# Attention and hyena stage of a hybrid block: another order within each attention step, four buffers for the hyena rows, and a step for the context keys

## The chip, the cores and the metric

The kernel runs on one core of a Trainium2 chip. The metric is device microseconds from start to end of the one launch; several runs are taken and their median stands for the kernel. Engines are named as in the profile: PE is TensorE, DVE is VectorE, ACT is ScalarE, POOL is GpSimd, SP is SyncE, which issues most of the DMAs.

## The reference

One layer of a diffusion backbone over 1024 latent tokens of width 1024, with 256 context tokens. A normalised and modulated input goes through one projection, whose columns feed neighbourhood attention (8 heads of 64, window 8 by 16 on a 16 by 64 grid, plus all context keys) and a two-step hyena long convolution; both are projected, gated and merged, and a SwiGLU network follows.

```python
h = modulate(rmsnorm(x, norm1_g[i]), sh1, sc1)
q, k, v, hv, hx1, hx2, gna, ghy = jnp.split(h @ w_in[i], IN_SPLITS, axis=-1)
y_na = neighbourhood_attention(to_heads(q), to_heads(k), to_heads(v),
                               to_heads(k_c), to_heads(v_c), na_rpb[i])
y_hy = hyena_mixer(hv, hx1, hx2, *hy_params)
x = x + g1 * gated_merge(gna, ghy, y_na, y_hy, w_na_o[i], w_hy_o[i], w_out[i])
# in neighbourhood_attention: s_nb = q_rot.k_band * scale + bias ; s_ctx = q.k_ctx * scale
#   p = softmax(concat(s_nb, s_ctx)) ; o = p_nb @ v_band + p_ctx @ v_ctx
# in gated_merge: m = sigmoid(g_na)*(y_na @ w_na_o) + sigmoid(g_hy)*(y_hy @ w_hy_o)
```

Everything is float32. The kernel gets that accuracy from TensorE by splitting each operand x into a high part (a cast by ACT, L178) and a low part (a subtraction by DVE, L179) and by three products (low weight by high x, high by low, high by high) for each product of the reference.

## The kernel before

The program runs through stages: modulation and first norm; the input projection, woven with the hyena filters and long convolutions; attention, woven with the rest of the projection and then with the hyena output projection; the merge and output projection; the SwiGLU network. The change touches the attention stage, which lies at 618 to 892 us of the span, and what is prepared for it.

**Items and steps.** Attention is cut into 32 items: 4 pairs of heads, 2 row blocks, 4 column blocks. Each item has 128 queries for two heads against 640 keys (384 of the window, 256 of the context). The generator `attention` makes one step for each item, and two more steps at the end. Step it issues, in this order on PE:

- scores of item it (`scores`, matmuls at L971 and L974, 12 of them, with 64-row tiles), into two PSUM tiles s_ps;
- turns of item it-1 (`turn`, L991): ten 128 by 128 transposes of the normalised probabilities pe into columns 0:1280 of the one PSUM tile pt_ps (a pool with a single buffer, 1536 columns of float32);
- values of item it-2 (`values`, L1005): 20 matmuls with 128 by 64 tiles from pts, the SBUF copy of the turned probabilities, into columns 1280:1408 of the same pt_ps;
- then a product: in the first 18 steps (items 0 to 17) 24 matmuls of the input projection into in_ps, after that 12 matmuls of the hyena output projection into hy_ps (both by `gemm`, L200).

DVE adds the bias to the scores and finds the maxima (L979, one instruction for each head), and scales by the reciprocal sum (L983, L984). ACT takes the exponentials (L980, two for an item, each followed by a read of its sum), copies the turned part of pt_ps to pts (L995 in `turned_out`), copies the values from pt_ps into a row of yrow (L1012 in `row`), and evicts the projection (L780). Both also do the splits of weights, queries, keys and rows (L178, L179). When a row block of yrow is full, it is split into yah and yal.

**What sets the order.** PE's instructions in this stage are pinned (`keep_in_program_order`), and so is each split passed a pin; the other instructions are placed on their engines by the framework's scheduler when the program is built. From then on each engine runs its list in order and waits on semaphores. Where an order is shown below, it is this built list. The main loop, from which each step's product follows its attention part, is

```python
while self.left:
    next(attention)
    next(proj)
...
for _ in attention:
    next(hyena, None)
```

**Preparation.** The generator `operands` loads and turns the next keys and queries (load, shuffle, two multiplications, an addition, then splits), one piece per step; six pieces run before the first item. The raw tiles have two buffers, and a load is issued when one is taken out.

**Hyena rows.** `hyena_out` reads eight rows yhraw (four channel blocks, two halves of the tokens) from memory through two buffers, splits them into yhh and yhl, which lie in the buffers that the projection's input occupied, and then runs eight output blocks f by two halves h, 12 matmuls each. The rows for the second half are split with a pin, the last two of them in the step of f=0, h=1, which is their first use.

Of the kernel before, what the change touches and what calls it, by code (L numbers as in the profile page):

```python
# [161 lines left out]
class Block:  # L162
# [696 lines left out]
    def attention(self, pool, kpool, prep, psums):  # L859
# [13 lines left out]

        jobs = [(nm, pr, h) for pr in range(4) for nm, h in (("k", 0), ("k", 1), ("kc", 0), ("q", 0), ("q", 1))]
        raws = []
# [39 lines left out]
        def keys(pr):  # L915
            tl = tiles[pr]
            tl["kr"] = [prep.tile([P, T], F32R, tag=n, name=n, bufs=2) for n in ("krh", "krl")]
            tl["kc"] = [prep.tile([P, TC], F32R, tag=n, name=n, bufs=2) for n in ("kch", "kcl")]
            for h in range(2):
                sl = slice(512 * h, 512 * h + 512)  # L920
                for n, x in enumerate(turned(sl, False)):
                    if n:
                        self.split(tl["kr"][0][:, sl], tl["kr"][1][:, sl], x)
                if h:
                    x = raws.pop(0)
                    fetch()
                    self.split(*tl["kc"], x[:, 0:TC])
                yield

        def queries(pr, h):  # L930
# [7 lines left out]
        def operands():  # L938
# [4 lines left out]
            yield from queries(0, 0)  # L943
            for pr in range(4):
                yield from queries(pr, 1)
                if pr < 3:
# [46 lines left out]
        def turned_out(pt):  # L993
            pts = pool.tile([P, 2, 640], F32, tag="pts", name="pts", bufs=2)
            nc.scalar.copy(pts.rearrange("p a b -> p (a b)"), pt[:, 0:1280])  # L995
            return pts
# [19 lines left out]
        prepared = operands()  # L1016
        for _ in range(6):
            next(prepared)
        yield
        pss, pst = psums()  # L1020
        one, two = {}, {}
        for it in range(len(items) + 2):
# [3 lines left out]
            pt = pst.tile([P, 1536], F32, tag="t", name="pt_ps")  # L1026
            pes = one.pop(it - 1, None)
            if pes:
                turn(pes, pt)
            if it >= 2:  # L1030
                values(two.pop(it - 2), pt, *items[it - 2])
            if pes:
                two[it - 1] = turned_out(pt)
            if it >= 2:
                row(pt, *items[it - 2])
            yield
# [11 lines left out]
    def hyena_out(self, pool, wpool, ps1):  # L1048

        nc, a = self.nc, self.a  # L1050
        yh = [pool.tile([P, 8, 512], F32R, tag=n, name=m).rearrange("p (c h) t -> p c (h t)", h=2)
              for n, m in (("hTh", "yhh"), ("hTl", "yhl"))]
        parts = [(c, h) for h in range(2) for c in range(4)]
        loaded = []

        def load(n):
            for c, h in parts[len(loaded):len(loaded) + n]:
                raw = self.stg.tile([P, 4, P], F32, tag="tm", name="yhraw").rearrange("p a b -> p (a b)")
                nc.sync.dma_start(raw, self.yhd[c][:, h * 512:(h + 1) * 512])
                loaded.append((c, slice(h * 512, (h + 1) * 512), raw))  # L1060
# [4 lines left out]

        load(2)
        yield
        for n in (0, 2):
            split(n)
            load(2)  # L1070
            yield
        split(4, self.tc.keep_in_program_order)
        load(2)
        w = self.weights(wpool, a["why"][0], 512)
# [125 lines left out]
    def run(self):  # L1200
        tc, nc, a = self.tc, self.nc, self.a
        with ExitStack() as top:
# [21 lines left out]
            with ExitStack() as s1:  # L1224
# [56 lines left out]
                prep, attk = side_pool("prep", bufs=2), side_pool("attk", bufs=1)  # L1281
                attention = self.attention(side_pool("att", bufs=2), attk, prep, psums)
                next(attention)
                for _ in range(AHEAD):
                    next(proj)
# [503 lines left out]
```

## Time and profile before

| | us |
|---|---|
| median of three runs | 1675.22 (1674.61 to 1676.2) |
| the profiled execution | 1675.84 |
| its span | 1674.1 |
| mean granted TensorE clock | 0.994 |

| engine | busy us | share |
|---|---|---|
| PE | 1646.1 | 98% |
| PE's weight loads | 1306.8 | 78% |
| DVE | 1229.4 | 73% |
| ACT | 696.6 | 42% |
| POOL | 150.0 | 9% |

The page lists busy time, then groups of instructions with their mean duration in ns and the idle time in front of them, with what ended it. A timeline row gives start, duration, engine, line, instruction, output and inputs, and in brackets the idle time ahead of it on its engine. Durations of matmuls that follow each other overlap in these rows, so distances between starts are used here for PE.

### The profile page before, as it was taken

The numbers are of one execution on the slowest core, as the hardware profiler recorded it, in microseconds if no ns is written. First come the engines' busy times: TensorE is split into PE (matmuls) and PEld (weight loads), VectorE is DVE, ScalarE is ACT, GpSimd is POOL, SyncE is SP. The second block draws the span as 40 slices with busy tenths as digits, with TensorE's granted clock in tenths as the row PEclk, the third lists the DMA queues.
The fourth block names the chain that finished last, engine by engine and source line by source line (L and its number), as shares of the span: only waits on it lengthen the run. The fifth ranks groups of instructions, "written<-read, shape, count | busy, mean of one in ns | idle before, by whom it ended". The sixth has DMA issues, their size and how long they took to land.

```text
span 1674.1 us, 22694 instructions
## 1 busy us (share of the span) xinstructions
PE 1646.1 (98%) x8168; PEld 1306.8 (78%) x8168; DVE 1229.4 (73%) x2079; ACT 696.6 (42%) x1217; POOL 150.0 (9%) x274
## 2 busy tenths in 40 slices
PE   8999999999999999999999999999999999999998
PEld 6777777777777778887787888888888888888886
DVE  5866799799999774647765868878866666489576
ACT  6553343222212146445553317632333333355455
POOL 1020001000000050202000001001100111000000
PEclk9999999999999999999999999999999999999999
DMA  9754455645555383446447514434432323395344
GB/s 363 246 173 162 162 165 177 212 159 182 194 179 189 128 249 105 133 129 180 160 143 271 176 41 179 141 119 133 142 104 95 101 102 119 114 360 193 100 121 157
DMA packets 107637, 274.37 MB, mean 164 GB/s; under 512 B 14687, under 2 KB 23811, under 8 KB 105221
## 3 DMA queue, kind: packets, MB, share of 16 engines
q1 hardware_dynamic: 87992, 212.14, 38.0%
q0 software_dynamic: 19168, 60.11, 10.6%
q8 instruction: 65, 1.06, 0.3%
q10 hardware_dynamic: 365, 0.67, 0.1%
q14 instruction: 47, 0.39, 0.1%
HBM read 205.48 MB, written 67.39 MB: 163 GB/s over the span
## 4 chain that ended last, share of the span: by engine, by line
PE 52%; issue 11%; DMA 2%; POOL 1%; DVE 1%; SPq 0%; ACT 0%; POOLq 0%; DVEq 0%
PE x_ps L1459 14%; PE z_ps L1459 6%; PE dx_ps L1647 6%; PE out_ps L1397 5%; PE in_ps L200 4%; PE dz_ps L1647 4%; PE hy_ps L200 3%; PE y_ps L1459 2%; PE dy_ps L1647 2%; PE na_ps L200 2%; PE pt_ps L1005 1%; PE pt_ps L991 1%; POOL v L909 1%; PE s_ps L971 1%; PE dft_ps L604 1%
## 5 line engine op out<-in xcount | busy, mean ns | idle before, releaser
L200 PE MATMUL in_ps<-hTh,wl 128*128 128x512 f32 x576 | 232.6, 404 | 1.6 <-ACT proj L780 1.6
L200 PE MATMUL in_ps<-hTh,wh 128*128 128x512 f32 x576 | 228.0, 396 | 0.0
L200 PE MATMUL in_ps<-hTl,wh 128*128 128x512 f32 x576 | 226.8, 394 | 0.0
L200 PEld LDWEIGHTS in_ps<-hTh,wl 128*128 128x128 f32 x576 | 108.2, 188 | 26.8 <-issue 3.1
L200 PEld LDWEIGHTS in_ps<-hTh,wh 128*128 128x128 f32 x576 | 108.2, 188 | 23.6 <-issue 0.3
L200 PEld LDWEIGHTS in_ps<-hTl,wh 128*128 128x128 f32 x576 | 108.3, 188 | 21.8
L178 ACT CAST wh<-wr 128x1024 fp32r<-128x1024 f32 (+1 forms) x60 | 52.7, 878 | 139.7 <-PE in_ps L200 106.4
L179 DVE TENSOR_TENSOR wl<-wr,wh 128x1024 fp32r<-128x1024 f32 (+1 forms) x60 | 60.4, 1007 | 66.9 <-ACT wh L178 66.7
L179 DVE TENSOR_TENSOR ol<-ws,oh 128x512 fp32r<-128x512 f32 x88 | 60.2, 688 | 50.6 <-ACT oh L178 50.5
L179 DVE TENSOR_TENSOR ol<-ar,oh 128x512 fp32r<-128x512 f32 x77 | 52.7, 687 | 39.1 <-ACT oh L178 39.0
L178 ACT CAST oh<-ar 128x512 fp32r<-128x512 f32 x77 | 47.9, 622 | 78.6 <-PE dx_ps L1647 29.2
L178 ACT CAST oh<-ws 128x512 fp32r<-128x512 f32 x88 | 54.6, 622 | 55.9 <-PE x_ps L1459 26.7
L979 DVE CUSTOM_DVE_ANT_0 pe<-s_ps,bias 128x640 f32<-128x640 f32 x64 | 50.6, 820 | 32.2 <-PE s_ps L974 32.2
L980 ACT ACTIVATE pe<-pe,mx 128x640 f32<-128x640 f32 x64 | 52.7, 824 | 48.4 <-DVE mx L979 48.3
L1647 PE MATMUL dx_ps<-ol,oh 128*128 128x512 f32 x176 | 68.7, 391 | 0.0
L1647 PE MATMUL dx_ps<-oh,ol 128*128 128x512 f32 x176 | 68.2, 390 | 0.4 <-DMA ar<-g 0.2
L1647 PE MATMUL dx_ps<-oh 128*128 128x512 f32 x176 | 68.5, 389 | 0.0
L604 PE MATMUL dft_ps<-a,matf 128*128 128x512 f32 x128 | 67.1, 605 | 1.1 <-ACT dec L509 0.5
L178 ACT CAST oh<-wr 128x512 fp32r<-128x512 f32 x70 | 43.3, 621 | 54.2 <-PE x_ps L1459 18.4
L179 DVE TENSOR_TENSOR ol<-wr,oh 128x512 fp32r<-128x512 f32 x70 | 47.9, 688 | 21.8 <-ACT oh L178 21.7
L1399 DVE TENSOR_TENSOR x<-x,out_ps 128x512 f32<-128x512 f32 x64 | 43.0, 685 | 20.3 <-PE out_ps L1397 19.4
L647 ACT COPY bp<-dft_ps 128x512 f32<-128x512 f32 x16 | 9.4, 588 | 104.1 <-PE dft_ps L606 100.2
(424 smaller groups left out, 4354.5 us busy)
## 6 DMA issues: line engine op xcount, KB each, us to landing
wr<-in_w SPq DMA_DIRECT2D x52, 512.0 KB, 3.5
ar<-g SPq DMA_DIRECT2D x77, 256.0 KB, 3.1
wr<-in_w_in SPq DMA_DIRECT2D x36, 512.0 KB, 3.8
matf<-in_dft_f SPq DMA_DIRECT2D x32, 384.0 KB, 3.6
bias<-in_rpb SPq DMA_DIRECT2D x64, 192.0 KB, 3.5
g<-t POOLq DMA_DIRECT2D x47, 256.0 KB, 3.0
w<-in_w SPq DMA_DIRECT2D x44, 256.0 KB, 5.4
x<-in_x SPq DMA_DIRECT2D x16, 512.0 KB, 7.8
```

The costliest lines, as they stand in the source:

```text
L178: pin(self.nc.scalar.copy(hi, src))
L179: pin(self.nc.vector.tensor_sub(lo, src, hi.bitcast(F32)))
L200: mm = nc.tensor.matmul(ps, ww[:, k * P:(k + 1) * P], xx[:, k, pos:pos + width], start=(i == 0), stop=(i == n - 1))
L604: nc.tensor.matmul(ps, m[:, 0], v.rearrange("p a b -> p (a b)"), start=True, stop=False)
L909: nc.gpsimd.dma_start(v[32 * r:32 * r + 32].rearrange("p (a b) f -> p a b f", b=4)[:, :, cb, :], vg[:, CBASE[cb]:CBASE[cb] + 32, fs].rearr ...
L971: pin(nc.tensor.matmul(ps[:, 512:896], qs[qq], kw[kk], start=(i == 0), stop=(i == 2)))
L979: nc.vector.tensor_tensor_reduce(pe, ps[:, 256:896], bt, -1.0, 3e38, ALU.add, ALU.min, mx[:, 0:1])
L980: nc.scalar.activation(pe, pe, AF.Exp, bias=mx[:, 0:1], scale=-1.0, accum_out=mx[:, 1:2])
L1397: nc.tensor.matmul(ps, gg[x][:, tk], ww[y][:, sl], start=(i == 0), stop=(i == n - 1))
L1399: nc.vector.tensor_add(x1[:, sl], x1[:, sl], ps)
L1459: mm = nc.tensor.matmul(ps, w[u][:, k * P:(k + 1) * P], x[v][:, k, :], start=(start and k == 0 and i == 0), stop=(stop and k == 3 and i == 2),
L1647: nc.tensor.matmul(ps[j], x[u][:, j * P:(j + 1) * P], w[v], start=(start and i == 0 and c == 0), stop=(stop and i == N - 1 and k == len(re ...
```

## The change

1. A step of attention is ordered scores, values and row copy, turns, copy of the turned part, product. The turned copy pts has one buffer instead of two.
2. The hyena rows go through four buffers, two of the old pool and two of the attention's own. The first four are loaded when attention begins, the tiles for their high and low parts are allocated a step later, and the third pair of rows is split without a pin a step earlier. The last pair stays pinned in the step of f=0, h=1.
3. The context keys of a pair are fetched one place later and split, pinned, in a piece of their own ahead of the second half of the queries; four pieces instead of six run before the loop, and one more after the PSUM pools are opened.

Lines move by a few: scores are L975 and L978, bias L983, exponentials L984, turns L995, turned copy L999, values L1009, row copy L1016 after the change.

```diff
@@ -871,7 +871,7 @@
         swap = [i ^ 16 for i in range(32)]
         tiles = {}
 
-        jobs = [(nm, pr, h) for pr in range(4) for nm, h in (("k", 0), ("k", 1), ("kc", 0), ("q", 0), ("q", 1))]
+        jobs = [(nm, pr, h) for pr in range(4) for nm, h in (("k", 0), ("k", 1), ("q", 0), ("kc", 0), ("q", 1))]
         raws = []
 
         def fetch():
@@ -921,11 +921,12 @@
                 for n, x in enumerate(turned(sl, False)):
                     if n:
                         self.split(tl["kr"][0][:, sl], tl["kr"][1][:, sl], x)
-                if h:
-                    x = raws.pop(0)
-                    fetch()
-                    self.split(*tl["kc"], x[:, 0:TC])
                 yield
+
+        def context(pr):
+            x = raws.pop(0)
+            fetch()
+            self.split(*tiles[pr]["kc"], x[:, 0:TC], pin)
 
         def queries(pr, h):
 
@@ -942,6 +943,9 @@
             yield from keys(0)
             yield from queries(0, 0)
             for pr in range(4):
+                context(pr)
+                if pr:
+                    yield
                 yield from queries(pr, 1)
                 if pr < 3:
                     values_of(pr + 1)
@@ -991,7 +995,7 @@
                     pin(nc.tensor.transpose(pt[:, at:at + P], pe[:, c * P:(c + 1) * P], self.ident))
 
         def turned_out(pt):
-            pts = pool.tile([P, 2, 640], F32, tag="pts", name="pts", bufs=2)
+            pts = pool.tile([P, 2, 640], F32, tag="pts", name="pts", bufs=1)
             nc.scalar.copy(pts.rearrange("p a b -> p (a b)"), pt[:, 0:1280])
             return pts
 
@@ -1014,10 +1018,11 @@
 
         items = [(pr, rb, cb) for pr in range(4) for rb in range(2) for cb in range(4)]
         prepared = operands()
-        for _ in range(6):
+        for _ in range(4):
             next(prepared)
         yield
         pss, pst = psums()
+        next(prepared)
         one, two = {}, {}
         for it in range(len(items) + 2):
             if it < len(items):
@@ -1025,14 +1030,12 @@
                 next(prepared, None)
             pt = pst.tile([P, 1536], F32, tag="t", name="pt_ps")
             pes = one.pop(it - 1, None)
+            if it >= 2:
+                values(two.pop(it - 2), pt, *items[it - 2])
+                row(pt, *items[it - 2])
             if pes:
                 turn(pes, pt)
-            if it >= 2:
-                values(two.pop(it - 2), pt, *items[it - 2])
-            if pes:
                 two[it - 1] = turned_out(pt)
-            if it >= 2:
-                row(pt, *items[it - 2])
             yield
 
     def pairs_done(self, pr, rb, cb):
@@ -1048,14 +1051,16 @@
     def hyena_out(self, pool, wpool, ps1):
 
         nc, a = self.nc, self.a
-        yh = [pool.tile([P, 8, 512], F32R, tag=n, name=m).rearrange("p (c h) t -> p c (h t)", h=2)
-              for n, m in (("hTh", "yhh"), ("hTl", "yhl"))]
+        yh = []
         parts = [(c, h) for h in range(2) for c in range(4)]
         loaded = []
 
         def load(n):
             for c, h in parts[len(loaded):len(loaded) + n]:
-                raw = self.stg.tile([P, 4, P], F32, tag="tm", name="yhraw").rearrange("p a b -> p (a b)")
+                if len(loaded) % 4 < 2:
+                    raw = self.stg.tile([P, 4, P], F32, tag="tm", name="yhraw").rearrange("p a b -> p (a b)")
+                else:
+                    raw = self.attpool.tile([P, 512], F32, tag="yhraw", name="yhraw")
                 nc.sync.dma_start(raw, self.yhd[c][:, h * 512:(h + 1) * 512])
                 loaded.append((c, slice(h * 512, (h + 1) * 512), raw))
 
@@ -1063,14 +1068,16 @@
             for c, sl, raw in loaded[n:n + 2]:
                 self.split(yh[0][:, c, sl], yh[1][:, c, sl], raw, *pin)
 
-        load(2)
+        load(4)
         yield
+        yh.extend(pool.tile([P, 8, 512], F32R, tag=n, name=m).rearrange("p (c h) t -> p c (h t)", h=2)
+                  for n, m in (("hTh", "yhh"), ("hTl", "yhl")))
         for n in (0, 2):
             split(n)
             load(2)
             yield
-        split(4, self.tc.keep_in_program_order)
-        load(2)
+        split(4)
+        yield
         w = self.weights(wpool, a["why"][0], 512)
         for f in range(8):
             if f == 7:
@@ -1279,8 +1286,10 @@
                 side_pool = lambda name, **kw: att.enter_context(tc.tile_pool(name=name, side="right", **kw))
                 psums = lambda: (side_pool("pss", bufs=2, space=PSUM), side_pool("pst", bufs=1, space=PSUM))
                 prep, attk = side_pool("prep", bufs=2), side_pool("attk", bufs=1)
-                attention = self.attention(side_pool("att", bufs=2), attk, prep, psums)
+                self.attpool = side_pool("att", bufs=2)
+                attention = self.attention(self.attpool, attk, prep, psums)
                 next(attention)
+                next(hyena)
                 for _ in range(AHEAD):
                     next(proj)
                 banks.close()
```

**First place: PE, the step whose pt_ps is number 7247, in the hyena part of the stage (item 22).** Before, from the last scores on:

```order
L974 MATMUL s_ps_7220<-kch_5808,qh_6179 128x256
L991 MATMUL pt_ps_7247<-ident_231,pe_7160 128x128 [waits DVE_49,PE_49,Activation_49]
L991 MATMUL pt_ps_7247<-ident_231,pe_7160 128x128 x4
L991 MATMUL pt_ps_7247<-ident_231,pe_7164 128x128 [waits DVE_49]
L991 MATMUL pt_ps_7247<-ident_231,pe_7164 128x128 x4
L1005 MATMUL pt_ps_7247<-pts_7193,vc_5804 64x128 x4
L1005 MATMUL pt_ps_7247<-pts_7193,v_5787 64x128 x6
L200 MATMUL hy_ps_7275<-yhh_6773,wl_7216 128x512 [waits DVE_49]
```

Now:

```order
L978 MATMUL s_ps_7220<-kch_5980,qh_6437 128x256
L1009 MATMUL pt_ps_7247<-pts_7196,vc_5976 64x128 [waits Activation_49]
L1009 MATMUL pt_ps_7247<-pts_7196,vc_5976 64x128 x3
L1009 MATMUL pt_ps_7247<-pts_7196,v_5959 64x128 x6
L995 MATMUL pt_ps_7247<-ident_231,pe_7153 128x128 [waits DVE_49,Activation_49]
L995 MATMUL pt_ps_7247<-ident_231,pe_7153 128x128 x4
L995 MATMUL pt_ps_7247<-ident_231,pe_7157 128x128 [waits DVE_49]
L995 MATMUL pt_ps_7247<-ident_231,pe_7157 128x128 x4
L200 MATMUL hy_ps_7275<-yhh_6756,wl_7216 128x512 [waits DVE_49]
```

The values are ahead of the turns, and the first turn of the step has a wait on ACT. The instruction of ACT that raises it to that count is the row copy of this same pt_ps; before, the count in the first turn was raised by a copy from the pt_ps of the step ahead.

**Second place: ACT, the same step.** wh is the high part of the next hyena weight, pe and mx are probabilities with their maxima and sums, yah the high part of a full row block. Before:

```order
L178 CAST wh_7358<-wr_7356 128x512 [waits DMAHW4_49,PE_49]
L980 ACTIVATE pe_7235,mx_7236<-pe_7235,mx_7236 128x640 [waits DVE_49]
L980 ACTIVATE pe_7239,mx_7240<-pe_7239,mx_7240 128x640 [waits DVE_49]
L995 COPY pts_7268<-pt_ps_7247 128x1280 [waits PE_49,Activation_49]
L1012 COPY yrow_6961<-pt_ps_7247 128x8x16
L178 CAST yah_6908<-yrow_6961 128x512 [waits Activation_49]
```

Now:

```order
L178 CAST wh_7358<-wr_7356 128x512 [waits DMAHW4_49,PE_49]
L984 ACTIVATE pe_7235,mx_7236<-pe_7235,mx_7236 128x640 [waits DVE_49]
L984 ACTIVATE pe_7239,mx_7240<-pe_7239,mx_7240 128x640 [waits DVE_49]
L1016 COPY yrow_6940<-pt_ps_7247 128x8x16 [waits PE_49]
L178 CAST yah_6892<-yrow_6940 128x512 [waits Activation_49]
L999 COPY pts_7271<-pt_ps_7247 128x1280 [waits PE_49,Activation_49]
```

The row copy (L1012, now L1016) moved ahead of the copy of the turned part and stands behind both exponentials of the step.

**Third place: ACT, the step of f=0, h=1 (item 19), where the last two hyena rows are split.** qh and qrh are high parts of queries, kch of context keys. Before:

```order
L178 CAST qh_6568<-qraw_6481 128x512 [waits PE_49]
L980 ACTIVATE pe_7011,mx_7012<-pe_7011,mx_7012 128x640 [waits DVE_49]
L980 ACTIVATE pe_7015,mx_7016<-pe_7015,mx_7016 128x640 [waits DVE_49]
L995 COPY pts_7044<-pt_ps_7023 128x1280 [waits PE_49,Activation_49]
L178 CAST qrh_6661<-qraw_6481 128x512 [waits DVE_49]
L1012 COPY yrow_6961<-pt_ps_7023 128x8x16
L178 CAST yah_6908<-yrow_5459 128x512
L178 CAST yhh_6773<-yhraw_6969 128x512 [waits DMAHW7_49]
L178 CAST yhh_6773<-yhraw_6971 128x512 [waits DMAHW0_49]
```

Now:

```order
L178 CAST qh_6833<-qraw_6723 128x512 [waits PE_49]
L984 ACTIVATE pe_6994,mx_6995<-pe_6994,mx_6995 128x640 [waits DVE_49]
L1016 COPY yrow_6940<-pt_ps_7010 128x8x16 [waits PE_49]
L178 CAST yah_6892<-yrow_5443 128x512
L984 ACTIVATE pe_6998,mx_6999<-pe_6998,mx_6999 128x640 [waits DVE_49]
L178 CAST kch_6634<-kcraw_6829 128x256 [waits DMAHW5_49]
L999 COPY pts_7034<-pt_ps_7010 128x1280 [waits PE_49,Activation_49]
L178 CAST qrh_6925<-qraw_6723 128x512 [waits DVE_49]
L178 CAST yhh_6756<-yhraw_6797 128x512 [waits DMAHW7_49]
L178 CAST yhh_6756<-yhraw_6799 128x512 [waits DMAHW0_49]
```

The row copy and yah moved between the two exponentials, a context-key split came in, and the two casts of hyena rows are still behind the turned copy and qrh.

## The prediction

> **What bounds the kernel now.** I read the page's first part, then busy time by stage (columns: length; PE, PEld, DVE, ACT, POOL busy with counts; granted clock; DMA share; GB/s), then what PE waits for.
>
> ```profile
> span 1674.1 us, 22694 instructions
> PE 1646.1 (98%) x8168; PEld 1306.8 (78%) x8168; DVE 1229.4 (73%) x2079; ACT 696.6 (42%) x1217; POOL 150.0 (9%) x274
> 618.00:782.00 164.00, 162.40 (x1137) 131.79 (x1137) 93.73 (x215) 88.91 (x156) 21.23 (x38) 1.00 0.43 132
> 782.00:892.00 110.00, 104.96 (x835) 83.41 (x833) 71.16 (x159) 60.69 (x115) 9.63 (x18) 0.97 0.52 159
> PE hy_ps L200 <- ACT yhh L178: 3.6, 1, 3.6
> PE in_ps L200 <- ACT proj L780: 1.6, 1, 1.6
> PE hy_ps L200 <- DVE yhl L179: 0.9, 1, 0.9
> ```
>
> PE sets the end: it is busy 98% of the span, and in the first 164 us of the attention steps it idles 1.6 us, all of it before the first scores. ACT and DVE have slack there as sums (89 and 94 of 164 us). So an edit counts here only by PE idle time, PE's own instructions or its clock. The second stretch idles 5.0 us, of which two waits of hyena_out for its input rows are 4.4. No row shows PE waiting for ACT or DVE inside an attention step. The change moves instructions of this stretch alone, and leaves the number of matmuls as it is.
>
> **Term 1, a new round trip PE-ACT-PE.** In the new order PE writes the values into pt_ps columns 1280:1408, ACT copies them out (the row copy), and only then may the turns write columns 0:1280 of the same tile: the order shown above has ACT's count in the wait of the first turn, and the ACT instruction that raises it is the row copy just listed. The trace of before shows that such waits go by tile, not by column (last columns: idle before, releaser):
>
> ```profile
> L995 ACT COPY pts<-pt_ps 128x1280 f32<-128x1280 f32 x32 | 38.9, 1215 | 2.2 <-PE pt_ps L1005 2.1
> ```
>
> The copy of the turned part, which reads 0:1280 only, waits for L1005, the values. The row copy reads after the values, so the new wait is real. Its price depends on what stands ahead of the row copy in ACT's order. A step of before (start, us, engine, line):
>
> ```profile
> 662.46 0.44 PE L971 MATMUL s_ps<-krh,qrl 64*128 64x384 f32 x2
> 663.54 1.31 PE L991 MATMUL pt_ps<-ident,pe 128*128 128x128 f32 x10
> 664.78 0.66 PE L1005 MATMUL pt_ps<-pts,vc 128*64 128x128 f32 x8
> 666.02 0.50 PE L200 MATMUL in_ps<-hTh,wl 128*128 128x512 f32 x1
> 664.51 0.83 ACT L980 ACTIVATE pe<-pe,mx 128x640 f32<-128x640 f32 x1 [1.35 <-DVE mx L979]
> 665.34 0.81 ACT L980 ACTIVATE pe<-pe,mx 128x640 f32<-128x640 f32 x1
> 666.20 1.23 ACT L995 COPY pts<-pt_ps 128x1280 f32<-128x1280 f32 x1
> 887.63 0.82 PE L1005 MATMUL pt_ps<-pts,v 128*64 128x128 f32 x12
> 888.38 0.50 PE L200 MATMUL hy_ps<-yhh,wl 128*128 128x512 f32 x1
> 888.50 0.27 ACT L1012 COPY yrow<-pt_ps 128x128 f32<-128x128 f32 x1 [2.77 <-PE pt_ps L1005]
> ```
>
> Scores take 663.54 - 662.46 = 1.08, values 666.02 - 664.78 = 1.24, so without a wait the turns would start at 2.32 after the step's start. The tail step shows the copy with nothing ahead of it: PE's next work starts at 888.38, the copy ends at 888.50 + 0.27 = 888.77; with 0.06 for the way back (my estimate, half the 0.12 from 888.38 to the copy's start) the loss is 0.45. In the built ACT order seven of the 31 steps with both values and turns have the copy so placed: 7 x 0.45 = 3.15; an eighth has a projection's eviction and a weight's cast ahead: 0.97.
>
> Behind both exponentials, as the second place of the order shows, the copy starts where ACT's next row starts, 666.20, and the turns at 666.20 + 0.27 + 0.06 = 666.53, which is 4.07 after the start: loss 1.75. Eight steps: 14.0, and 0.31 for a context-key cast in one of them. The other cases:
>
> ```profile
> 680.98 0.45 PE L971 MATMUL s_ps<-krh,qrl 64*128 64x384 f32 x2
> 683.78 0.18 ACT L980 ACTIVATION_READ_ACCUMULATOR pe<-pe,mx 128x1 f32 x1
> 684.39 0.83 ACT L980 ACTIVATE pe<-pe,mx 128x640 f32<-128x640 f32 x1 [0.43 <-DVE mx L979]
> 685.22 1.21 ACT L995 COPY pts<-pt_ps 128x1280 f32<-128x1280 f32 x1
> 842.53 0.45 PE L971 MATMUL s_ps<-krh,qrl 64*128 64x384 f32 x2
> 846.40 1.21 ACT L995 COPY pts<-pt_ps 128x1280 f32<-128x1280 f32 x1
> 764.99 1.13 ACT L178 CAST yhh<-yhraw 128x512 fp32r<-128x512 f32 x2
> qraw<-qk SPq DMA_DIRECT2D x8, 256.0 KB, 3.5
> ```
>
> Between the exponentials (five steps): first one done 683.96, + 0.33, less 680.98 and 2.32 = 0.99, so 4.95. Behind both, with a weight's split ahead (five hyena steps): 846.40 + 0.33 - 842.53 - 2.32 = 1.88, so 9.4. Item 3, with a query split between the bias additions: 685.22 + 0.33 - 680.98 - 2.32 = 2.25. Four crowded steps remain. Item 16 has all four hyena casts ahead of the exponentials: 1.75 + 2 x 1.13 less 0.3 that the bias additions cover = 3.7. Items 17 and 18 have an eviction or a weight's cast more, about 0.6 each: 2.35 twice. In item 20 DVE's order puts the shuffle of a query tile ahead of the bias addition, and that tile's load (3.5 us to landing) is issued only after the split that frees its buffer; laid out by hand, 4.06. Sum of the four 12.46.
>
> Term 1: 3.15 + 0.97 + 14.31 + 4.95 + 9.4 + 2.25 + 12.46 = **47.5 us**. Lower bound: all the steps behind both exponentials cost as those between them, 8 x 0.76 + 5 x 0.89 = 10.5 less.
>
> **Term 2, hyena rows.** Two waits and the clock (rows of the two timelines; then windows, PE's busy time first, granted clock third from the end):
>
> ```profile
> 786.42 0.51 PE L200 MATMUL hy_ps<-yhh,wl 128*128 128x512 f32 x1
> 792.96 0.51 PE L200 MATMUL hy_ps<-yhh,wl 128*128 128x512 f32 x1
> 798.23 0.80 PE L200 MATMUL hy_ps<-yhh,wl 128*128 128x512 f32 x1 [3.59 <-ACT yhh L178]
> 799.88 0.79 PE L200 MATMUL hy_ps<-yhl,wh 128*128 128x512 f32 x1 [0.85 <-DVE yhl L179]
> 806.84 0.50 PE L200 MATMUL hy_ps<-yhh,wl 128*128 128x512 f32 x1
> 797.00:798.00 1.00, 0.00 (x0) 0.00 (x0) 1.00 (x2) 1.00 (x3) 0.00 (x0) 0.86 0.57 221
> 798.00:799.00 1.00, 0.77 (x1) 0.29 (x1) 1.00 (x3) 0.70 (x2) 0.00 (x0) 0.50 0.07 26
> 796.36 0.61 ACT L178 CAST qrh<-qraw 128x512 fp32r<-128x512 f32 x1
> 797.56 1.14 ACT L178 CAST yhh<-yhraw 128x512 fp32r<-128x512 f32 x2
> ```
>
> One step takes 792.96 - 786.42 = 6.54; the next 806.84 - 792.96 = 13.88. It loses 7.34: 4.44 of waits and 2.90 of slow clock, after 3.59 us idle. With four buffers the last two rows are there early, but their split is still pinned to this step, and ACT's order (third place above) has it behind the turned copy (1.21) and a query cast (0.61). The turned copy itself now starts only after the turns, when the product starts too. The first of the two casts ends 1.21 + 0.61 + 0.57 = 2.39 after that; PE wants it after six matmuls of 0.23 = 1.4: 1.0 us of wait. The DVE halves come behind a query's subtraction and a scaling, as at 799.88: about 1.4 more. So 2.4 of 7.34 stay, with no clock drop: **-4.9 us**, bounds 0 and -7.3. The four casts that the change takes ahead of this step now stand in items 16 and 17, and term 1 holds them. The extra loads have DMA engines that are 0.43 busy in the stretch, and their rows are wanted over 100 us after they are issued: 0.
>
> **Term 3, fewer changes of shape on PE.** Turns run straight into the product (128 by 128 tiles both), where before the values (128 by 64) stood between:
>
> ```profile
> 627.92 1.31 PE L991 MATMUL pt_ps<-ident,pe 128*128 128x128 f32 x10
> 628.99 0.47 PE L200 MATMUL in_ps<-hTh,wl 128*128 128x512 f32 x1
> 629.30 0.39 PE L200 MATMUL in_ps<-hTl,wh 128*128 128x512 f32 x1
> 666.36 0.39 PE L200 MATMUL in_ps<-hTl,wh 128*128 128x512 f32 x1
> 638.20 0.19 PEld L200 LDWEIGHTS in_ps<-hTh,wl 128*128 128x128 f32 x1 [0.17 <-issue]
> ```
>
> The first step has no values: turns take 628.99 - 627.92 = 1.07 to the product, against 664.78 - 663.54 = 1.24 to values; the product's first matmul 0.31 against 666.36 - 666.02 = 0.34. Scores (64-row tiles) now meet values, where they met turns; both change the shape, so I add nothing. 0.15 of the 0.20 for 30 steps: **-4.5 us**, bounds 0 and -6. [...]
>
> **Small terms.** The context keys of the first pair are now split just ahead of the first scores, behind an eviction and a weight's cast: their cast and subtraction lengthen the 1.6 us wait there by about 0.3. For the later pairs they are a step of their own, in slack, but for the 0.31 above. One copy buffer instead of two: a step's values are done before its turned copy starts, so nothing waits: 0. The clock: idle of 1.6 us kept 1.00 (first window), 3.59 us cost 2.90. Items 16 and 20 idle 3.7 and 4.06; I count one drop, **+2.9**.
>
> **Sum.** +47.5 - 4.9 - 4.5 + 0.3 + 2.9 = +41.3 on the profiled run's 1675.84 (span 1674.1 and 1.7 around it); the median shown, 1675.22, is 0.6 lower: 1675.2 + 41.3 = **1716.5 us**.
>
> **Rivals.** (a) *Faster*: the row copy is done before the turns are reached, because PE's waits resolve without it or ACT is ready ahead. Then terms 2 to 4 stay: -4.9 - 4.5 + 0.3 = -9.1, 1666 us. For it: no wait on ACT in any step of before. Against: the copy cannot start before the values end, and even the tail's row loses 0.45. It turns to a gain only below 9.1/31 = 0.29 per step. 0.06. (b) *Every copy straight behind the values*: 31 x 0.45 = 14.0, net +4.9, 1680 us. Against: ACT's order is fixed in the program, and over half of the steps have both exponentials first. 0.08. (c) *The clock falls in all four crowded steps*, three drops more at 2.9: 1725 us. For it: the row at 0.50 after 3.59 idle; against: 2.35 is nearer the 1.6 that kept 1.00. [...] 0.16. (d) *Four buffers do not shorten the hyena wait*, since its split stays pinned: 1721 us, inside the forecast's range.
>
> **How the numbers follow.** Forecast with (d) 0.70, (c) 0.16, (b) 0.08, (a) 0.06. Low end: two thirds of term 1's 10.5, no clock drop, the rest of terms 2 and 3 (2.4 + 1.5) in full: 1716.5 - 13.8, about 1702. High end: (c) with terms 2 and 3 halved, 1725.2 + 4.7, about 1730. Within 0.2% (3.4 us, about what a measurement of this kernel can tell from no change) needs (b) a little cheaper: 0.02. Faster only by (a): 0.06; slower 0.92.
>
> **What would show it.** Right: a PE wait for ACT's row copy before the first turn in some 31 steps, 0.45 with the copy alone and 1.7 to 1.9 behind both exponentials, 45 to 50 us in all; the first stretch's PE idle from 1.6 to about 22; the wait for yhh at 1 instead of 3.6. Wrong: no such wait (term 1 gone), or one of equal small size in all steps (b); clock 0.5 in several stretches (c); the 3.6 still there (d).

## The result, and the profile after

| | before | after |
|---|---|---|
| median, us | 1674.61 (1672.71 to 1676.2, 5 runs) | 1725.33 (1722.24 to 1726.54, 5 runs) |
| span of the profiled execution | 1674.1 | 1723.5 |
| mean granted clock | 0.994 | 0.989 |

The change makes the kernel slower: 1.0302 times the time, 95% interval 1.0289 to 1.0316, 50.7 us by the medians. The forecast was 1716.5.

PE has nearly the same busy time, 1649.8 us instead of 1646.1, in a span that is 49.4 us longer. So 45.7 of the 49.4 us are idle time of PE. Busy times after, from the page:

```profile
PE 1649.8 (96%) x8168; PEld 1312.0 (76%) x8168; DVE 1230.0 (71%) x2079; ACT 697.6 (40%) x1217; POOL 150.3 (9%) x274
```

What PE waits for, after (engine, tile and line, releaser: us in total, times, longest):

```profile
PE pt_ps L995 <- ACT yrow L1016: 41.4, 31, 3.3
PE s_ps L978 <- DVE kcl L179: 5.7, 1, 5.7
PE in_ps L200 <- ACT proj L780: 1.4, 1, 1.4
PE s_ps L978 <- ACT kch L178: 1.2, 1, 1.2
PE hy_ps L200 <- DVE yhl L179: 1.1, 1, 1.1
PE hy_ps L200 <- ACT yhh L178: 1.1, 1, 1.1
```

The first row is new and is the round trip that the prediction named: 31 waits of the first turn for the row copy, 41.4 us. The second and fourth rows are new too, 6.9 us at the first scores, and the prediction had 0.3 there. The two hyena waits fell from 4.4 to 2.2.

An ordinary step shows the price. Timeline rows of PE, and then of ACT, in item 22 after (start, us, engine, line, idle before and releaser):

```profile
848.41 0.45 PE L975 MATMUL s_ps<-krh,qrl 64*128 64x384 f32 x2
850.00 0.82 PE L1009 MATMUL pt_ps<-pts,v 128*64 128x128 f32 x12
852.57 1.31 PE L995 MATMUL pt_ps<-ident,pe 128*128 128x128 f32 x10 [1.75 <-ACT yrow L1016]
856.58 0.45 PE L975 MATMUL s_ps<-krh,qrl 64*128 64x384 f32 x2
```

```profile
851.47 0.81 ACT L984 ACTIVATE pe<-pe,mx 128x640 f32<-128x640 f32 x1
852.28 0.24 ACT L1016 COPY yrow<-pt_ps 128x128 f32<-128x128 f32 x1
```

The values end at 850.82. The row copy starts at 852.28, because the second exponential stands ahead of it on ACT, and the turns start at 852.57. Apart from a few crowded ones, the 31 waits fall into the classes of the prediction: 0.36 to 0.37 with nothing ahead of the copy, 0.78 to 0.79 between the exponentials, 1.59 to 1.76 behind both.

In the attention stage the granted clock falls to 0.50 in five places after (for 10.24 us at the first scores and for 3.41 us in each of items 16, 17, 20 and 24), and in one before (for 6.83 us at the hyena rows). A window of after shows the second of the four later ones (PE's busy time first, granted clock third from the end):

```profile
805.00:807.00 2.00, 2.00 (x6) 1.52 (x6) 0.00 (x0) 1.23 (x1) 1.25 (x3) 0.50 1.04 258
```

### The profile page after: what moved, and what is told of

Read it like the earlier page. It is cut to its first block, busy times and chain, and to the rows that moved or that the text cites. A ratio compares the mean times of both kernels' runs of the same rounds, so it can differ in the third digit from the quotient of the medians.

```text
span 1723.5 us, 22693 instructions
## 1 busy us (share of the span) xinstructions
PE 1649.8 (96%) x8168; PEld 1312.0 (76%) x8168; DVE 1230.0 (71%) x2079; ACT 697.6 (40%) x1217; POOL 150.3 (9%) x274
## 4 chain that ended last, share of the span: by engine, by line
PE 68%; issue 15%; DVE 7%; ACT 4%; DMA 4%; POOL 1%; SPq 1%; POOLq 0%; DVEq 0%; ACTq 0%
PE x_ps L1468 14%; PE in_ps L200 12%; PE z_ps L1468 6%; PE dx_ps L1656 6%; PE out_ps L1406 5%; PE dz_ps L1656 3%; PE pt_ps L995 3%; PE hy_ps L200 2%; PE dft_ps L604 2%; PE in_ps L811 2%; ACT pe L984 2%; PE y_ps L1468 2%; PE dy_ps L1656 2%; PE na_ps L200 2%; PE dft_ps L606 1%
## 5 line engine op out<-in xcount | busy, mean ns | idle before, releaser
L995 PE MATMUL pt_ps<-ident,pe 128*128 128x128 f32 x320 | 44.7, 290 | 41.4 <-ACT yrow L1016 41.4
L983 DVE CUSTOM_DVE_ANT_0 pe<-s_ps,bias 128x640 f32<-128x640 f32 x64 | 50.5, 820 | 37.1 <-PE s_ps L978 37.1
L995 PEld LDWEIGHTS pt_ps<-ident,pe 128*128 128x128 f32 x320 | 36.5, 146 | 49.0 <-ACT yrow L1016 48.8
L984 ACT ACTIVATE pe<-pe,mx 128x640 f32<-128x640 f32 x64 | 52.6, 822 | 43.4 <-DVE mx L983 43.4
```

The lines of the kernel that those rows point to most:

```text
L983: nc.vector.tensor_tensor_reduce(pe, ps[:, 256:896], bt, -1.0, 3e38, ALU.add, ALU.min, mx[:, 0:1])
L984: nc.scalar.activation(pe, pe, AF.Exp, bias=mx[:, 0:1], scale=-1.0, accum_out=mx[:, 1:2])
L995: pin(nc.tensor.transpose(pt[:, at:at + P], pe[:, c * P:(c + 1) * P], self.ident))
```

## The experiments

All ratios are to runs of the kernel before on the same chip and in the same session, with 95% intervals. The medians of those runs lie between 1674.6 and 1675.9 us.

### The round trip: row copy after the turns

```diff
             if it >= 2:
                 values(two.pop(it - 2), pt, *items[it - 2])
-                row(pt, *items[it - 2])
             if pes:
                 turn(pes, pt)
                 two[it - 1] = turned_out(pt)
+            if it >= 2:
+                row(pt, *items[it - 2])
             yield
```

> The change with one line moved: the row copy is issued after the turns and the turned copy instead of ahead of them. Theory (the round trip): the first turn no longer waits for ACT, so the 41.4 us of PE waits for the row copy go to 0 and with them the four clock drops in the later items (about 1.6 each, 6.4): 1725.3 - 47.8 = about 1677 us; the 5.7 us wait for kcl at the first scores stays. Rival (ACT is simply crowded in the new arrangement, the dependency only shows it): PE waits of over 20 us for ACT stay under another name, time 1700 or more.

Measured: 1680.0 us, ratio 1.0024 (1.0011 to 1.0037). One moved line gives back 45 of the 51 us. No PE wait for the row copy is left; these are the longest waits around the stage:

```profile
PE s_ps L978 <- DVE kcl L179: 5.3, 1, 5.3
PE hy_ps L200 <- ACT yhh L178: 2.5, 1, 2.5
```

The crowding rival falls: ACT has the same instructions, and no wait of PE for ACT comes near 20 us. A step of the same kind as item 22 above, item 26, now begins and ends so:

```profile
846.54 0.45 PE L975 MATMUL s_ps<-krh,qrl 64*128 64x384 f32 x2
852.88 0.45 PE L975 MATMUL s_ps<-krh,qrl 64*128 64x384 f32 x2
```

From scores to scores it takes 852.88 - 846.54 = 6.34. After, it was 856.58 - 848.41 = 8.17, so the round trip costs 1.83 in a step of this kind (item 26 itself took 8.18 after). Before, item 26 took 6.56 (its scores start at 842.53, those of item 27 at 849.09, in the row below), so values ahead of turns are themselves a gain of 0.22. The four later clock drops are gone with the waits, but for one of 3.4 us at the hyena rows. The hyena waits are 3.3 us instead of 2.2. Neither explains the 3 us by which the median lies above the theory's 1677: the profiled execution has both and took 1677.2, the shortest of the ten. Where the others lose more is not shown.

```profile
849.09 0.44 PE L971 MATMUL s_ps<-krh,qrl 64*128 64x384 f32 x2
```

### What stands ahead of the row copy

```diff
-            nc.scalar.copy(dst, pt[:, 1280:1408].rearrange("p (r c) -> p r c", c=16))
+            with self.tc.high_priority():
+                nc.scalar.copy(dst, pt[:, 1280:1408].rearrange("p (r c) -> p r c", c=16))
```

> The change with the row copy given high priority, nothing else: in the built ACT order it now stands right behind the values in eight steps, as before, and between the two exponentials in the other 23, in none behind both. Theory (the price of a step's wait is what stands ahead of the copy on ACT): waits 8 x 0.4 + 23 x 0.8 plus about 4 for the steps with hyena casts ahead = 26 us instead of 41.4, no clock drop in steps with 0.8, so about 1725.3 - 15 - 6 = 1704 us. Rival (the price is the way PE-ACT-PE itself, the order on ACT does not matter): waits stay at 40, 1725.

Measured: 1704.7 us, ratio 1.0175 (1.0157 to 1.0192), within a microsecond of what was expected.

```profile
PE pt_ps L995 <- ACT yrow L1017: 25.5, 31, 1.9
```

The wait is still there 31 times, but costs 25.5 us instead of 41.4, since no row copy stands behind both exponentials any more. So the price of the wait is ACT's order, on top of a floor of 0.37 for the copy and the way to ACT and back.

### The attention order alone, and the context keys alone

The order alone is the kernel before with the order of the change; the context keys alone are the kernel before with `context(pr)` and the other fetch order.

```diff
             if it >= 2:
                 values(two.pop(it - 2), pt, *items[it - 2])
+                row(pt, *items[it - 2])
             if pes:
+                turn(pes, pt)
                 two[it - 1] = turned_out(pt)
-            if it >= 2:
-                row(pt, *items[it - 2])
             yield
```

(with `turn(pes, pt)` taken away from its place ahead of the values)

> The kernel before with the attention order alone (scores, values and row, turns, copy, product); two copy buffers, hyena rows and context keys as before. Theory: the round trip costs about 41 us of PE waits for the row copy also without the other two parts, two to five clock drops of 1.6, less 3.9 for fewer changes of tile shape: about 1716 us, 1711 to 1721. Rival (the crowding by moved hyena casts and key splits makes half of the loss): waits of 20 to 30 us, 1695 to 1705.

Measured: 1710.0 us, ratio 1.0204 (1.0177 to 1.0232), so about 34 us; the wait for the row copy is 38.3 us in 31 steps. That is 1 us below the range expected. The hyena rows are as before here, and still their waits are short:

```profile
PE pt_ps L991 <- ACT yrow L1012: 38.3, 31, 2.3
PE hy_ps L200 <- ACT yhh L178: 1.0, 1, 1.0
```

PE now arrives late itself, and the casts are done by then: 3.6 became 1.0 without any change to the rows. (The wait for yhl is 1.5, where it was 0.9.)

```diff
-        jobs = [(nm, pr, h) ... (("k", 0), ("k", 1), ("kc", 0), ("q", 0), ("q", 1))]
+        jobs = [(nm, pr, h) ... (("k", 0), ("k", 1), ("q", 0), ("kc", 0), ("q", 1))]
...
             for pr in range(4):
+                context(pr)
+                if pr:
+                    yield
                 yield from queries(pr, 1)
```

> The kernel before with the context keys' own step alone. Theory: a PE wait for kcl of about 5 us appears at the first scores, with half clock behind it: 1674.6 + 8 to 10 = about 1683 us. Rival (it needs the early hyena loads to be late): no such wait, 1675.

Measured: 1684.9 us, ratio 1.0051 (1.0034 to 1.0069). The wait at the first scores appears without any change to the hyena loads:

```profile
PE s_ps L978 <- DVE kcl L179: 6.1, 1, 6.1
```

The step of item 0 takes 16.1 us from scores to scores instead of 8.5. That is not the whole cost: in item 19 a later pair's kcl stands on DVE ahead of yhl, the two hyena waits are 5.9 us instead of 4.4 with 10.2 us at half clock instead of 6.8, and the step takes 15.7 us instead of 12.9.

The chain of waits of the changed kernel says why (start, us, what; the steps up to the first scores that end):

```profile
620.00 0.70 DVE krl L179
...
620.72 3.34 DMA kraw<-qk
...
626.78 1.22 DVE wl L179
628.00 0.34 DVE kcl L179
...
628.38 0.79 PE s_ps L978 x3
```

The split of the first pair's context keys is pinned, but the scheduler has put the second pair's key pieces ahead of it on DVE. One of these waits for a load that can start only when a raw buffer comes free, at 620.72, after the other piece's split. The raw context keys hold the second buffer until kcl is done. So kcl, which needs 0.34 us, ends at 628.34, and the first scores of the stage wait for it.

The reverse, the changed kernel with the context keys put back:

> The change with the context keys put back where they were before (fetch order, split inside the keys' piece, six pieces ahead of the loop); attention order and hyena rows as changed. Theory (the context split itself: kcl stands on DVE behind a later pair's key piece whose load was issued late): the waits of PE for kch and kcl (1.2 and 5.7) vanish with the slow clock behind them (2.9), 1725.3 - 9 = about 1716 us. Rival (the four hyena loads at the start of attention delay the key loads): the wait for kcl stays, 1725.

Measured: 1713.7 us, ratio 1.0225 (1.0199 to 1.0252). The waits for kch and kcl are gone, and 12 us of the 51 with them. But another wait is longer at the same place, the first product's for an eviction:

```profile
PE in_ps L200 <- ACT proj L780: 4.2, 1, 4.2
```

With the old context keys and without the hyena part, in the order alone, it was 1.0. So the rival had a point that the expectation did not give it: the hyena part does cost something there, though not by way of kcl.

### The hyena rows

The hyena part alone, with the old order and the old context keys (one copy buffer):

> The hyena rows alone: order of the attention step and context keys as before, four buffers, third pair of rows split early, last pair pinned in its step. Theory of the prediction: the waits for yhh and yhl go from 4.4 to 2.4 us and the clock drop of 2.9 behind them goes: -4.9, 1670 us. Rival (from the runs so far, where 3.3 us of waits stay with the order's round trip gone): -2 with the clock drop still there, 1673; or nothing, 1675.

Measured: 1680.9 us, ratio 1.0036 (1.0025 to 1.0047). It is a loss of 6 us, and neither expectation had that.

```profile
PE hy_ps L200 <- ACT yhh L178: 3.6, 1, 3.6
PE in_ps L200 <- ACT proj L780: 3.4, 1, 3.4
PE hy_ps L200 <- DVE yhl L179: 0.9, 1, 0.9
```

The hyena waits are what they were before, 3.6 and 0.9. Four buffers do not help a split that is pinned to the step of its use. And the wait ahead of the first product went from 1.6 to 3.4, with 6.8 us at half clock that begin within it: the step of item 0 takes 12.7 us instead of 8.5, which is 4.2 of the 6.

The SP queue points to the cause (start, us, line). First before, then the hyena part alone:

```profile
579.60 0.80 SPq L865 DMA_DIRECT2D rope<-in_rope  x2
592.11 0.33 SPq L882 DMA_DIRECT2D kcraw<-kc  x1
613.79 0.32 SPq L882 DMA_DIRECT2D kcraw<-kc  x1
```

```profile
577.90 0.81 SPq L865 DMA_DIRECT2D rope<-in_rope  x2
590.71 0.33 SPq L1061 DMA_DIRECT2D yhraw<-yh  x1
591.13 0.40 SPq L882 DMA_DIRECT2D kcraw<-kc  x1
614.36 0.32 SPq L882 DMA_DIRECT2D kcraw<-kc  x1
```

Counted from the load of rope, the second context-key load leaves at 34.2 before and at 36.5 now. A row load stands ahead of the first context-key load, which leaves 13.2 after rope instead of 12.5, and the preparation is a chain of loads, shuffles and splits, each waiting for a raw buffer, so it passes the delay on. ACT casts the second context keys ahead of the eviction that PE waits for. PE comes to the first scores at the same distance from rope, 38.8 in both, and waits for what is late.

To show that it is the loads, they were to be issued after the fourth step of attention:

```diff
                 next(attention)
-                next(hyena)
...
+                n = 0
                 while self.left:
                     next(attention)
                     next(proj)
+                    n += 1
+                    if n == 4:
+                        next(hyena)
```

> As the run with the hyena rows alone, but their first four loads are issued after the fourth step of attention instead of at its start. Theory (the early loads put the first key loads back by some 2 us, which makes the wait before the first product 3.4 instead of 1.6 and lets the clock fall): the wait is back at 1.6 with full clock, and the time back at that of before within 2 us, 1675; the waits for yhh and yhl stay 3.6 and 0.9. Rival (the longer wait there is a matter of when PE arrives, not of the loads): 3.4 and half clock stay, 1680.

Measured: 1682.5 us, ratio 1.0038 (1.0023 to 1.0052), no better; the wait is 4.3. The edit did not do what it says: the loads are not pinned, and the scheduler put two of them on SP where they had been, one ahead of the first context-key load.

```profile
593.06 0.33 SPq L1061 DMA_DIRECT2D yhraw<-yh  x1
593.78 0.33 SPq L882 DMA_DIRECT2D kcraw<-kc  x1
```

So this run decides nothing on the loads; the pinned one below does.

### The clock

> The changed kernel unaltered, a second profile. [...] Rival (the clock falls by the length of a wait alone): the same four items show 0.5.

Measured: 1722.1 us, one run. The waits are nearly the same (40.7 us for the row copy instead of 41.4), and a slow clock follows partly other ones: items 16, 17, 18 and 26 and the hyena rows in item 19, where in the first profile it was items 16, 17, 20 and 24. (There are five later drops against four, but at the first scores 6.8 us at half clock against 10.2; the span, 1720.3, is shorter, so the number of drops is not what sets the two apart.) Ten turns take 1.31 us at full clock, so a longer duration in the row shows a slow clock; behind item 18 of the second execution it begins only at the end of the turns, at 814.67. In the first profile of the changed kernel (items 17 and 18), then in the second (items 17, 18, 24 and 26):

```profile
803.38 1.56 PE L995 MATMUL pt_ps<-ident,pe 128*128 128x128 f32 x10 [2.25 <-ACT yrow L1016]
816.32 1.31 PE L995 MATMUL pt_ps<-ident,pe 128*128 128x128 f32 x10 [2.25 <-ACT yrow L1016]
```

```profile
800.51 1.95 PE L995 MATMUL pt_ps<-ident,pe 128*128 128x128 f32 x10 [2.25 <-ACT yrow L1016]
813.48 1.31 PE L995 MATMUL pt_ps<-ident,pe 128*128 128x128 f32 x10 [2.24 <-ACT yrow L1016]
866.66 1.31 PE L995 MATMUL pt_ps<-ident,pe 128*128 128x128 f32 x10 [2.50 <-ACT yrow L1016]
882.84 2.35 PE L995 MATMUL pt_ps<-ident,pe 128*128 128x128 f32 x10 [1.75 <-ACT yrow L1016]
```

The length of the wait does not decide: 2.25 is followed by a slow clock in item 17 and not in item 18 of the first execution, and in the second execution 2.50 is not while 1.75 is. The slow stretches of the first profile begin at 623.38, 790.64, 804.29, 835.01 and 869.14; the first lasts 10.24 us and the other four 3.41 each, and the one of before lasts 6.83.

The two hyena waits of item 19 come out differently too. They are 1.09 and 1.14 us in both executions, and half clock follows them in the second and not in the first. A window of the second execution that holds both and ends where the clock falls (PE's busy time is the second length, the clock third from the end):

```profile
824.91:828.33 3.42, 1.18 (x5) 0.72 (x5) 3.42 (x8) 1.60 (x4) 0.00 (x0) 1.00 0.24 77
```

PE idles 3.42 - 1.18 = 2.24 us in it. What decides besides the wait is left open here.

### Versions without the losses

The kernel before with only the late row copy (values, turns, turned copy, row copy):

> The kernel before with the order values, turns, turned copy, then row copy, and nothing else changed (two copy buffers, hyena rows and context keys as before). Theory: 0.21 us less for each of 30 steps, no wait for ACT's row copy, the first-scores wait at 1.6 and the hyena waits as before: 1674.6 - 6.3 = about 1668 us. Rival (PE reaches the hyena rows earlier and only waits longer there): the 2.7 of the steps after item 18 is kept but half of the first 18 steps' 3.5 goes into the wait for yhh, 1670 or more.

Measured: 1671.6 us, ratio 0.9969 (0.9955 to 0.9983). The projection steps are shorter by 0.2 each as in the first experiment, but the wait for yhh grew and the clock falls behind it (0.50 from 792 to 794 us; items 19 and 20 take 22.3 us instead of 20.4), so some 2 of the 6.3 us are lost there, which is what the rival had in mind:

```profile
PE hy_ps L200 <- ACT yhh L178: 4.2, 1, 4.2
```

The late row copy with old context keys, four hyena buffers and `split(6)` without its pin, loads early:

```diff
                 if f == 0 and h:
-                    split(6, self.tc.keep_in_program_order)
+                    split(6)
```

> Values, turns, turned copy, then row copy (no wait of the turns on ACT); context keys as before; four buffers for the hyena rows and all their splits without a pin. Theory: 0.21 for each of 30 steps (6.3) from the new order and the whole 7.3 of the hyena wait: 1674.6 - 13.6 = about 1661 us. Rival (the two unpinned casts make other steps late instead, as the first four do in items 16 and 17): only the 6.3, 1668 us.

Measured: 1670.0 us, ratio 0.9973 (0.9959 to 0.9986). The waits for yhh and yhl are gone, but the wait ahead of the first product is 3.1 us, with 3.4 us at half clock behind it, and 2.2 us of new waits stand in items 19 and 20 (1.4 of them values that wait for a row copy), as the rival had it. The time is 9 us above the theory's. The same with the loads moved in the text alone:

> The combined version (values, turns, turned copy, row copy; context keys as before; four hyena buffers, no split pinned) with the hyena loads issued after the fourth step. Theory: the wait before the first product goes from 3.1 to about 1.6 and its half clock goes, so 3 to 4 us less than the 1670.0 of the version with early loads: about 1666.5 us. Rival (the loads do not matter): 1670.

Measured: 1667.6 us, ratio 0.9949 (0.9932 to 0.9965); its loads stood on SP as early as in the other unpinned run, and the wait was 4.5, so the loads do not explain its time; the interval overlaps that of the version ahead of it. With the first four loads pinned as well:

```diff
+                d = nc.sync.dma_start(raw, self.yhd[c][:, h * 512:(h + 1) * 512])
+                if len(loaded) < 4:
+                    self.tc.keep_in_program_order(d)
-                nc.sync.dma_start(raw, self.yhd[c][:, h * 512:(h + 1) * 512])
```

> The combined version with the first four hyena loads pinned behind the fourth step; in the built order of SP they now really stand behind the first biases of the steps (in the two runs with unpinned late loads two of them still stood around the first context-key load, since only the program text had moved). Theory (loads ahead of the key loads put the preparation back): the second context-key load is issued some 34.5 us after the rope load as in the kernel before instead of 36.5 to 38.5, the wait before the first product is at most 1.6 with full clock, and the time is 3 to 5 us below the 1667.6 of the version without the pin: about 1663.5 us. Rival: preparation and wait (3 to 4.5) stay, 1667.5.

Measured: 1665.0 us, ratio 0.9942 (0.9921 to 0.9963), the fastest of all, though its interval overlaps the one just above.

```profile
580.49 0.80 SPq L865 DMA_DIRECT2D rope<-in_rope  x2
593.16 0.33 SPq L882 DMA_DIRECT2D kcraw<-kc  x1
614.91 0.32 SPq L882 DMA_DIRECT2D kcraw<-kc  x1
```

```profile
PE in_ps L200 <- ACT proj L780: 0.5, 1, 0.5
619.24:781.40 162.16, 161.61 (x1165) 133.58 (x1166) 96.00 (x219) 91.22 (x160) 21.54 (x39) 1.00 0.46 144
781.40:882.00 100.60, 97.29 (x808) 79.44 (x804) 67.56 (x155) 57.55 (x110) 8.60 (x16) 1.00 0.51 162
```

With no row load among them, the second context-key load leaves at 34.4 after rope, the wait is 0.5, and the clock is 1.00 through the stage. The step of item 0 takes 7.41 us, and 13.25 in the version without the pin. In this pair of versions nothing else differs, so the mechanism of the loads is shown; the size of its effect on the time (1667.6 against 1665.0) is inside the intervals. All the profiles with the old context keys agree: where row loads stand ahead, the load leaves at 36.5 to 38.5 and the wait is 3.1 to 4.5 (five), where none does, at 34.2 to 34.7 and the wait is 0.5 to 1.6 (four).

## Why the prediction was right or wrong

**The whole.** Forecast 1716.5, measured 1725.3, on the side and with the mechanism that was named. That the number came as near is in part luck: term 1 was 6.1 us too large in its waits, and the wait at the first scores 6.6 too small. What is left is mostly the clock, by an estimate some 9.5 us (half of the 18.9 us that PE worked at half clock) against the 2.9 forecast. The parts by themselves cost 34 (order), 8.5 (context keys) and 6 us (hyena rows) by their ratios times 1675, though the prediction had the last two at +0.3 and -4.9. That these sum to 49 of the 51 does not mean that they add: the wait of 3.4 ahead of the first product, which with the slow clock behind it makes most of the hyena part's loss, is 1.4 in the whole change.

**Term 1, the round trip: right, size 47.5 against 41.4.** That the dependency goes by the whole tile, that ACT's order sets the price, and the count of 31 held. The prices were 0.45, 0.99 and 1.75 to 1.88, and the waits 0.37, 0.78 and 1.59 to 1.76. The wait stands ahead of the first of the ten turns, which writes columns 0:128, so it is not a matter of the neighbouring columns. A step's distance is longer than the wait by about 0.08 (1.83 for a wait of 1.75 in item 22), so the first and last classes are nearly right as losses. The rest of the excess came from the crowded steps and item 3: 12.46 for items 16, 17, 18 and 20, which measured 3.25 + 2.25 + 2.25 + 2.08 = 9.8, and 2.25 for item 3, which measured 1.60. Item 20's 4.06, laid out by hand from a late load, measured 2.08. Item 24, put at 1.88, measured 2.50. In the steps of items 0 to 17 PE idles 24.5 us where about 22 were forecast, but 6.9 of them are at the first scores.

**Term 2, hyena rows: wrong, and the step that failed is the split's cover.** The 2.4 us of waits that were to remain did remain (2.2), but by luck and not for the reason given. In the second execution of the changed kernel a clock drop followed them all the same. With the hyena part alone they are 4.5 as before; with the order alone they are 1.0 and 1.5. It is the round trip that lets ACT catch up, so the gain was bought with the waits of term 1 and could not be added to them as a saving of this edit. Rival (d) was the true one for the edit by itself.

**The sentence that the extra loads cost 0: wrong.** It looked at the DMA engines' share and at when the rows are wanted, and not at what stands behind a load that waits in SP's queue. The first context-key load stood behind one, the preparation came 2.3 us later, and the first product's wait grew by 1.8 with a slow clock behind it. That makes 4.2 of the 6 us of the part.

**Small terms, context keys: wrong, 0.3 against about 8.5.** The step that failed is the costing of the split by its own instructions. What counted was its place on DVE, behind another pair's key piece whose load had no buffer yet; the prediction places it by ACT's order alone. Nor were the later pairs' context keys free: with the context keys alone, one of them stands on DVE ahead of the hyena rows of item 19, and the waits there are longer.

**Term 3: right in kind, 4.5 against 6.3.** With the round trip taken away each step is shorter by 0.2, the upper of the two values worked out, and the sum is just beyond the bound of 6. Where scores now meet values nothing was lost: in item 26 the values start 1.09 after the scores, and before, the turns started 1.10 after them. That the changes of shape make the gain is argued from the order; no run varies them alone.

**The clock: 1 drop against 4 and a long one.** Four late drops of 3.41 us at half clock cost about 1.7 each, 6.8, by the same estimate (matmuls of the product start 0.43 us apart from 805.16 to 807.30 and 0.23 apart behind that), and the one at the first scores is 10.24 us at half clock, 5.0 of it while PE was idle anyway. The one of before (6.83 us long) is gone. Rival (c) was half right: items 16, 17, 20 and 24 in one profile, 16, 17, 18 and 26 and the hyena rows in the next. That its 1725 us is the measured time is chance, since it has three more drops at 2.9 and nothing at the first scores.

**Rivals (a) and (b)** fell with the first row of the waits; (b) is what high priority for the copy moves towards, 25.5 us of waits, and would have needed the copy ahead of the first exponential as well.

## What to carry to other kernels

Before an engine's order is changed, ask for each tile who last touched it, on any engine and in any column: here a reader on ACT came between two writers on PE, the second writer waited for what stood ahead of the reader on ACT (31 waits, 41.4 us), and moving the reader behind the second writer took the wait away. An instruction that was moved or pinned cost what stood ahead of it on each engine it runs on (kcl, 0.34 us long, held the first scores up for 5.7), and a load what stood behind it in its queue (behind a row load the second context-key load left 2.3 us later), so the built orders of all of these are to be read, not its duration. Savings that come from a stall elsewhere are not to be added to it: with the order alone PE came late, and the wait for yhh was 1.0 us instead of 3.6 with the rows unchanged.

## What was not expected of the hardware

The clock fell behind a wait of 1.75 us in one execution and did not behind one of 2.50 us in the same. In the first profile it fell for 3.41 us four times and for 10.24 us once. Two executions of one kernel with nearly the same waits differed: half clock stood in items 16, 17, 20 and 24 of one and in items 16, 17, 18, 19 and 26 of the other. Each 3.41 us at half clock cost about 1.7 us here by the estimate above.
